# Order of small fp32 products on TensorE in a hybrid decoder step

## The chip, the cores and the metric

The kernel runs on one core of a Trainium2 chip. Its time is what one execution takes on the device, in microseconds (us); the profile is that of one execution, and TensorE, VectorE, ScalarE, GpSimd and SyncE stand in it as PE (PEld for its weight loads), DVE, ACT, POOL and SP.

## What is computed

One layer of a decoder for 1024 new prompt tokens and 64 sampled tokens (8 sequences of 8): a normalised input goes through one projection, whose columns feed an RWKV-7 recurrence (4 heads of 64), a short convolution and a stick-breaking attention (8 heads of 64); then an output projection, an MLP of width 4096 and a gated embedding. The sampled tokens continue 8 cached states and attend to 512 past positions each, kept in pages of 128 rows that a page table names. The parts that bear on the change:

```python
def wkv7_scan(r, decay, k, v, a_vec, b_vec, s0):
    def step(s, inp):
        r_t, w_t, k_t, v_t, a_t, b_t = inp
        sa = jnp.einsum('bhvk,bhk->bhv', s, a_t)
        s = (s * w_t[:, :, None, :] + sa[..., None] * b_t[:, :, None, :]
             + v_t[..., None] * k_t[:, :, None, :])
        y = jnp.einsum('bhvk,bhk->bhv', s, r_t)
        return s, y
...
        z = jnp.einsum('bqhd,bkhd->bhqk', q_blk.astype(jnp.float32), kf) * scale + bias_f
        mask = k_pos[None, :] < q_pos[:, None]
        log_beta = jnp.where(mask, jax.nn.log_sigmoid(z), -jnp.inf)
        log_keep = jnp.where(mask, jax.nn.log_sigmoid(-z), 0.0)
        later = lax.cumsum(log_keep, axis=3, reverse=True) - log_keep
        wts = jnp.exp(log_beta + later)
        return jnp.einsum('bhqk,bkhd->bqhd', wts, vf)
```

## The kernel before

The large products (projections, MLP) split every fp32 operand into a high and a low part and add three full-array products (L169 to L171, L775 to L777, L1262 to L1264). The work that the change touches is done in plain fp32 products whose operands have 64 rows, 64 columns or both. A product `matmul(out, w, x)` loads `w` into the array. The partitions (rows of memory) on which `w` and `x` lie are the array's rows, the partitions of `out` are its columns. So a product whose operands lie on partitions 0 to 63 and whose result goes to partitions 64 to 127 uses one quarter of the array.

The prompt's recurrence runs in chunks of 64 tokens. `wkv_local` does the work of two neighbouring chunks (e = 0, 1) that needs no state, in steps that each fill a PSUM bank and have it evacuated by ScalarE or VectorE: masked products of keys and queries (L507, head halves s = 0, 1 on opposite row halves, all 128 columns), transposes (L514, L522), then four products per chunk, one for each head, in L529, L541, L548, L557, L558 and L569. In L529 to L558 chunk 0 and chunk 1 lie on opposite rows and write opposite halves of a bank; in L569 heads alternate between the column halves. `wkv_chain` carries the state from chunk to chunk: L614 prepares the state's additions, L622 (128 rows) and L624 (64 rows, with the state) accumulate the output of a chunk head by head, L630 carries the state on. `hp(h)` is the half of the partitions that head h uses, `es(e)` and `ks(e)` are the halves that chunk e uses. Two generators of `wkv_local` and one of `wkv_chain` are advanced in turn by `run`; each `wkv_local` generator takes its banks from `banks(3)` or from `banks(4)`, that is, one bank each, and the next taker of a bank waits until it has been read out.

`wkv_sample_chunk` treats the 64 sampled tokens as one chunk with 8 states: it transposes the 8 states of two heads at a time (L698), runs `wkv_local` with a single chunk, adds the states' share of the output (L707 and, 8 per head, L710), and makes the new states (L719, L722, L731, transposes in L738).

`decode` is the paged attention of the sampled tokens: two sequences (s = 0, 1) at a time, whose results go to opposite halves of a bank. Pages are gathered by POOL into rotating buffers (5 for keys, 6 for values), key pages are transposed (L1100), and the scores (L1106, 4 products of 512 columns per sequence, accumulated), the weights (a scan on VectorE) and the values (L1130, one product for each of 4 pages, and L1131 for the new rows, accumulated) follow. L1072 makes the scores of the new rows.

The kernel text gives the order of the program; a scheduler lays the instructions of each engine into a queue from it, taking what it reckons to be ready, so that products of other parts (the query, key and value projection beside the recurrence, the convolution and the first attention beside the sampled chunk, the MLP's first part beside the decode attention) stand between those of a stage. [...]

Of the kernel before, what the change touches and what calls it, by code (L numbers as in the profile page):

```python
# [32 lines left out]
NB = 8  # L33
# [7 lines left out]
PAGES = 4  # L41
# [7 lines left out]
def hybrid_step(ctx: ExitStack, tc: tile.TileContext, I, O):  # L49
# [402 lines left out]
    def hp(h):  # L452
        return slice(64 * (h % 2), 64 * (h % 2) + 64)
# [4 lines left out]
    def j2(t, n=128):  # L458
        return t[:, :n].rearrange("p (j c) -> p j c", j=2)
# [3 lines left out]
    def wkv_local(cs, res, local, sample=False):  # L463
# [5 lines left out]
        def es(e):  # L469
            return slice(64 * e, 64 * e + 64)  # L470
# [28 lines left out]
        mk = mfull[:, 1 if sample else 0].rearrange("p a t -> p (a t)")[:, None, None, :].to_broadcast([128, ne, 2, 128])  # L499
        for s in range(2):  # L500
            hs = slice(64 * s, 64 * s + 64)
            pab = local()
            p4 = pab.rearrange("p (e j c) -> p e j c", e=2, j=2)
            for e in E:
                for j in range(2):
                    ra = ar[hs, e, j, 0:2] if e == 0 else ar[hs, e, j, 2:0:-1]
                    PE.matmul(p4[:, e, j, :], bk[hs, e, j].rearrange("p a t -> p (a t)"), ra, start=True, stop=True)  # L507
            V.tensor_mul(AB[:, 0:ne, s:4:2, 64:192], p4[:, 0:ne], mk)
        yield
# [16 lines left out]
        px = local()  # L526
        for e in E:
            for h in range(4):
                PE.matmul(h4(px)[es(e), h, :], AB[ks(e), e, h, 128:192], UV[ks(e), e, h, :], start=True, stop=True)  # L529
# [3 lines left out]
        if not sample:  # L533
            LM = kp.tile([128, 4, 64], F32, name="LM", bufs=1 if sample else 2)
            for e in E:
                V.tensor_mul(LM[es(e)], AB[es(e), e, :, 128:192], lvl[es(e), None, :].to_broadcast([64, 4, 64]))
            yield
            py = local()
            for e in E:
                for h in range(4):  # L540
                    PE.matmul(h4(py)[es(e), h, :], LM[es(e), h, :], TT[es(e), h, 1, :], start=True, stop=True)  # L541
            Y1 = kp.tile([128, 4, 64], F32, name="Y1", bufs=1 if sample else 2)
            S.copy(Y1, h4(py))
            yield
            pd = local()
            for e in E:
                for h in range(4):
                    PE.matmul(h4(pd)[es(e), h, :], Y1[es(e), h, :], TT[es(e), h, 0, :], start=True, stop=True)  # L548
            V.tensor_add(TT[:, :, 0], h4(pd), TT[:, :, 0])
            yield  # L550
        else:
            yield
        psv = local()
        p4 = h4(psv, 512)
        for e in E:
            for h in range(4):
                PE.matmul(p4[es(e), h, 0:64], TT[es(e), h, 0, :], X[es(e), h, :], start=True, stop=True)  # L557
                PE.matmul(p4[es(e), h, 64:128], TT[es(e), h, 0, :], UV[es(e), e, h, :], start=True, stop=True)  # L558
        for e in E:
# [4 lines left out]
        Rm = kp.tile([128, ne, 2, 64], F32, name="Rm", bufs=1 if sample else 3)  # L564
        FT = kp.tile([128, ne, 2, 64], F32, name="FT", bufs=1 if sample else 3)
        for e in E:
            prf = local()
            for h in range(4):
                PE.matmul(j2(prf, 256)[hp(h), h // 2, :], Wm[es(e), h, :], AB[es(e), e, h, 0:128], start=True, stop=True)  # L569
            V.tensor_add(Rm[:, e], j2(prf, 256)[:, :, 64:128], R(e))  # L570
            if not sample:
                V.tensor_add(FT[:, e], j2(prf, 256)[:, :, 0:64], id128[:, None, :].to_broadcast([128, 2, 64]))
# [33 lines left out]
    def wkv_chain(c, AB, UV, Wm, Rm, FT):  # L606
# [11 lines left out]
        for e in range(2):  # L618
            St = state[0]
            for h in range(4):  # L620
                o = p4[hp(h), e, h // 2, :]
                PE.matmul(o, UV[:, e, h, :], AB[:, e, h, 64:128], start=True, stop=St is None)  # L622
                if St is not None:
                    PE.matmul(o, St[hp(h), h // 2, :], Rm[hp(h), e, h // 2, :], start=False, stop=True)  # L624
            if St is None:
                state[0] = PG[:, e]
                continue
            pf = chain()
            for h in range(4):
                PE.matmul(j2(pf)[hp(h), h // 2, :], FT[hp(h), e, h // 2, :], St[hp(h), h // 2, :], start=True, stop=True)  # L630
            Sn = kp.tile([128, 2, 64], F32, name="St", bufs=3)
            for j in range(2):
                V.scalar_tensor_tensor(Sn[:, j, :], j2(pf)[:, j, :], pcs[:, j, c + e:c + e + 1], PG[:, e, j, :],
                                       op0=ALU.mult, op1=ALU.add)
            state[0] = Sn
            yield
# [13 lines left out]
    def wkv_prompt_chunks():  # L650
# [16 lines left out]
        steps = chains()  # L667
        run(locals_(range(0, 16, 4), banks(3), 0), locals_(range(2, 16, 4), banks(4), 5), steps, steps)
        St = state[0]
# [8 lines left out]
    def wkv_sample_chunk(bank):  # L678
# [12 lines left out]
        for j in range(2):  # L691
            pt = bank()
            s_in = sp.tile([128, NB, 64], F32, name="s_in", tag="um", bufs=2)
            for s in range(2):
                hs = slice(64 * s, 64 * s + 64)
                SP.dma_start(s_in[hs], st[:, 2 * j + s].rearrange("b v k -> v b k"))
                for b in range(NB):
                    PE.matmul(pt[hs, b * 64:b * 64 + 64], s_in[hs, b, :], ident[hs, hs], start=True, stop=True)  # L698
            S.copy(S0[:, j].rearrange("p b v -> p (b v)"), pt)
# [4 lines left out]
        py = bank()  # L704
        for h in range(4):
            o = j2(py)[hp(h), h // 2, :]
            PE.matmul(o, UV[:, 0, h, :], AB[:, 0, h, 64:128], start=True, stop=False)  # L707
            for b in range(NB):
                q = slice(b * NJ, b * NJ + NJ)
                PE.matmul(o[:, q], S0[hp(h), h // 2, b, :], Rm[hp(h), 0, h // 2, q], start=False, stop=b == NB - 1)  # L710
        S.copy(Yg, j2(py))
        run(wkv_out(NP, 64, Yg, bank))
        for j in range(2):
            pg, pf = bank(), bank()
            for s in range(2):
                h = 2 * j + s
                um = sp.tile([128, NB, 64], F32, name="um", tag="um", bufs=2)
                V.tensor_mul(um, UV[:, 0, h, None, :].to_broadcast([128, NB, 64]), bm)
                PE.matmul(pg[hp(h), :], AB[:, 0, h, 0:64], um.rearrange("p b v -> p (b v)"), start=True, stop=True)  # L719
                bmk = sp.tile([64, NB, 64], F32, name="bmk", bufs=1)  # L720
                V.tensor_mul(bmk, AB[0:64, 0, h, None, 0:64].to_broadcast([64, NB, 64]), bm[0:64])
                PE.matmul(pf[hp(h), :], Wm[0:64, h, :], bmk.rearrange("p b k -> p (b k)"), start=True, stop=True)  # L722
# [4 lines left out]
            pn = bank()  # L727
            for s in range(2):
                hs = slice(64 * s, 64 * s + 64)
                for b in range(NB):  # L730
                    PE.matmul(pn[hs, b * 64:b * 64 + 64], FT[hs, b, :], S0[hs, j, b, :], start=True, stop=True)  # L731
            V.tensor_add(GS, pn.rearrange("p (b k) -> p b k", b=NB), GS)
            V.tensor_mul(GS, GS, pcs[:, j, 16:24, None].to_broadcast([128, NB, 64]))
            po = bank()
            for s in range(2):
                hs = slice(64 * s, 64 * s + 64)
                for b in range(NB):
                    PE.matmul(po[hs, b * 64:b * 64 + 64], GS[hs, b, :], ident[hs, hs], start=True, stop=True)  # L738
# [268 lines left out]
    def decode():  # L1007
# [61 lines left out]
        pzn = pdc()  # L1069
        for b in range(NB):  # L1070
            for r in range(4):
                PE.matmul(pzn[64 * (b % 2):64 * (b % 2) + 64, (b // 2) * NS:(b // 2) * NS + NS], Qb[:, r, b, :],  # L1072
                          kT[:, r, :], start=r == 0, stop=r == 3)
# [16 lines left out]
        for bp in range(4):  # L1090
# [11 lines left out]
            pz = pdc()  # L1102
            for s in range(2):
                b = 2 * bp + s
                for r in range(4):
                    PE.matmul(pz[64 * s:64 * s + 64, :], Qb[:, r, b, :], kts[s][:, r, :], start=r == 0, stop=r == 3)  # L1106
            beta = dp.tile([128, W_], F32, name="dbeta", bufs=2)
# [17 lines left out]
            po = pdc()  # L1125
            for s in range(2):
                q = slice(64 * s, 64 * s + 64)
                for n in range(PAGES):
                    vp = page("vpg", vrows, 2 * bp + s, n, 6)
                    PE.matmul(po[q, :], wT[:, n, q], vp, start=n == 0, stop=False)  # L1130
                PE.matmul(po[q, :], wT[:NS, 4, q], vd.rearrange("t r c -> t (r c)"), start=False, stop=True)  # L1131
            ow = dp.tile([128, 8, 64], F32, name="ow", bufs=2)
# [255 lines left out]
```

## Time and profile before

| | us |
|---|---|
| median of 3 runs | 1829.38 |
| lowest and highest of them | 1828.57, 1829.54 |
| the profiled execution | 1823.9 |
| its span | 1822.2 |

The granted TensorE clock of the profiled execution was 0.985 on average. In the lines of a timeline that follow, the columns are the start in us from the span's start, the length in us from the first start to the last end, the engine, the line of the kernel, the operation, result and operands, then the rows and columns of the array used, the moving operand, and the number of records that were merged. The end of a product is modelled, so one lasts longer than the distance to the next start; what a line costs is read from its start to the start of the next line.

### The profile page before, as it was taken

The numbers are of one execution on the slowest core, as the hardware profiler recorded it, in microseconds if no ns is written. First come the engines' busy times: TensorE is split into PE (matmuls) and PEld (weight loads), VectorE is DVE, ScalarE is ACT, GpSimd is POOL, SyncE is SP. The second block draws the span as 40 slices with busy tenths as digits, with TensorE's granted clock in tenths as the row PEclk, the third lists the DMA queues.
The fourth block names the chain that finished last, engine by engine and source line by source line (L and its number), as shares of the span: only waits on it lengthen the run. The fifth ranks groups of instructions, "written<-read, shape, count | busy, mean of one in ns | idle before, by whom it ended". The sixth has DMA issues, their size and how long they took to land.

```text
span 1822.2 us, 29843 instructions
## 1 busy us (share of the span) xinstructions
PE 1761.2 (97%) x11933; PEld 1560.7 (86%) x11933; DVE 1016.2 (56%) x1634; ACT 703.2 (39%) x1283; POOL 480.6 (26%) x412
## 2 busy tenths in 40 slices
PE   6998899999999799999999999999999999999998
PEld 5898888888998777888886665799999999998998
DVE  6267944443566669878763334435555555548532
ACT  5633223222433557565532223334222322225421
POOL 4123321212200243222235433242122212212310
PEclk9999999999989899999999999999999999999999
DMA  5135366423513653333245443523222222221121
GB/s 177 49 121 147 100 154 163 101 71 108 154 50 93 194 168 99 120 119 109 86 120 174 126 126 105 187 70 93 93 72 91 80 84 93 70 87 60 53 72 38
DMA packets 195149, 194.87 MB, mean 107 GB/s; under 512 B 57729, under 2 KB 166945, under 8 KB 194882
## 3 DMA queue, kind: packets, MB, share of 16 engines
q1 hardware_dynamic: 189890, 176.18, 32.4%
q0 software_dynamic: 5120, 16.78, 3.1%
q8 instruction: 94, 1.54, 0.4%
q14 instruction: 45, 0.37, 0.1%
HBM read 155.92 MB, written 36.98 MB: 106 GB/s over the span
## 4 chain that ended last, share of the span: by engine, by line
PE 80%; DVE 9%; DMA 4%; issue 3%; ACT 3%; POOL 1%; SPq 0%; ACTq 0%; DVEq 0%; POOLq 0%
PE b L169 12%; PE b L170 12%; PE b L171 12%; PE b L1262 6%; PE b L1264 6%; PE b L1263 6%; PE b L775 2%; PE b L776 2%; PE b L777 2%; PE b L1130 2%; PE b L895 1%; PE b L1106 1%; DVE base_Q L281 1%; DVE keep L875 1%; DVE nl L1189 1%
## 5 line engine op out<-in xcount | busy, mean ns | idle before, releaser
L159 POOL TENSOR_TENSOR wl<-wr,wh 128x1024 fp32r<-128x1024 f32 (+1 forms) x116 | 289.8, 2517 | 594.0 <-ACT wh L158 593.8
L170 PE MATMUL b<-nl,wh 128*128 128x288 f32 (+1 forms) x960 | 316.7, 330 | 2.2 <-DVE nl L1189 2.2
L169 PE MATMUL b<-nh,wh 128*128 128x288 f32 (+1 forms) x960 | 317.4, 331 | 0.9 <-DVE x L1234 0.9
L171 PE MATMUL b<-nh,wl 128*128 128x288 f32 (+1 forms) x960 | 315.9, 329 | 0.0
L158 ACT CAST wh<-wr 128x1024 fp32r<-128x1024 f32 (+1 forms) x178 | 177.9, 1041 | 265.5 <-PE b L1263 164.1
L1265 DVE TENSOR_TENSOR x<-b,x 128x288 f32<-128x288 f32 (+1 forms) x384 | 200.8, 531 | 140.5 <-PE b L1264 140.3
L1262 PE MATMUL b<-ah,wh 128*128 128x288 f32 (+1 forms) x768 | 256.9, 335 | 5.8 <-DVE x L1265 5.3
L1264 PE MATMUL b<-ah,wl 128*128 128x288 f32 (+1 forms) x768 | 252.3, 329 | 0.0
L1263 PE MATMUL b<-al,wh 128*128 128x288 f32 (+1 forms) x768 | 251.8, 328 | 0.0
L170 PEld LDWEIGHTS b<-nl,wh 128*128 128x128 f32 x960 | 180.9, 188 | 14.9 <-DVE nl L1189 3.1
L169 PEld LDWEIGHTS b<-nh,wh 128*128 128x128 f32 x960 | 180.9, 188 | 14.7 <-issue 1.6
L171 PEld LDWEIGHTS b<-nh,wl 128*128 128x128 f32 x960 | 181.0, 189 | 14.5 <-issue 2.7
L1262 PEld LDWEIGHTS b<-ah,wh 128*128 128x128 f32 x768 | 144.4, 188 | 23.3 <-DVE x L1265 8.2
L1264 PEld LDWEIGHTS b<-ah,wl 128*128 128x128 f32 x768 | 144.4, 188 | 12.2 <-issue 2.4
L1263 PEld LDWEIGHTS b<-al,wh 128*128 128x128 f32 x768 | 144.4, 188 | 9.1 <-issue 0.8
L775 PE MATMUL b<-wh,h_hi 128*128 128x256 f32 x432 | 128.8, 298 | 0.0
L776 PE MATMUL b<-wl,h_hi 128*128 128x256 f32 x432 | 127.9, 296 | 0.0
L777 PE MATMUL b<-wh,h_lo 128*128 128x256 f32 x432 | 127.1, 294 | 0.0
L169 PE MATMUL b<-h_hi,wh 128*128 128x384 f32 (+1 forms) x336 | 116.2, 346 | 1.9 <-ACT xs L330 1.2
L1247 DVE SCALAR_TENSOR_TENSOR r<-b,rb 128x288 f32<-128x288 f32 (+1 forms) x96 | 51.1, 534 | 117.2 <-PE b L171 114.3
L875 DVE TENSOR_TENSOR_SCAN keep<-keep,onesq 128x128 f32<-128x128 f32 (+3 forms) x64 | 97.6, 1528 | 31.9 <-ACT keep L874 31.5
L170 PE MATMUL b<-h_lo,wh 128*128 128x384 f32 (+1 forms) x336 | 113.8, 339 | 0.3 <-DVE h_lo L201 0.3
(375 smaller groups left out, 3427.7 us busy)
## 6 DMA issues: line engine op xcount, KB each, us to landing
wr<-in_w_up SPq DMA_DIRECT2D x62, 512.0 KB
wr<-in_w_down SPq DMA_DIRECT2D x62, 512.0 KB
wr<-in_w_in SPq DMA_DIRECT2D x26, 512.0 KB
wr<-in_w_out SPq DMA_DIRECT2D x16, 512.0 KB
xt<-in_x_prompt SPq DMA_DIRECT2D x8, 512.0 KB
stk_s<-sth SPq DMA_DIRECT2D x32, 128.0 KB
stk_s<-stl SPq DMA_DIRECT2D x32, 128.0 KB
out<-nat SPq DMA_DIRECT2D x16, 256.0 KB
```

Of the source, the lines that this page charges most:

```text
L158: S.copy(wh[:, flat], raw[:, :n * ncol])
L159: (sub or G).tensor_sub(wl[:, flat], raw[:, :n * ncol], f(wh[:, flat]))
L169: PE.matmul(ps[:, :n], wh[:, k, c], a, start=(k == 0), stop=False)
L170: PE.matmul(ps[:, :n], wh[:, k, c], b, start=False, stop=False)
L171: PE.matmul(ps[:, :n], wl[:, k, c], a, start=False, stop=(k == nk - 1))
L775: PE.matmul(o, a, w[0][:, k, :], start=(k == 0), stop=False)
L776: PE.matmul(o, a, w[1][:, k, :], start=False, stop=False)
L777: PE.matmul(o, b, w[0][:, k, :], start=False, stop=(k == 7))
L1262: PE.matmul(ps[:, :n], wh[:, k, c], a, start=k == 0, stop=False)
L1263: PE.matmul(ps[:, :n], wh[:, k, c], b, start=False, stop=False)
L1264: PE.matmul(ps[:, :n], wl[:, k, c], a, start=False, stop=k == 1)
L1265: V.tensor_add(p.x[:, m, t0:t0 + n], ps[:, :n], p.x[:, m, t0:t0 + n])
```

## The change

The order of products changes, so that neighbours use different row halves, different column halves or both. The products themselves and what they compute stay.

- `wkv_local`: L507 alternates between the row halves, with one bank for each (in the sampled chunk it stays one half after the other); L529, L541, L548, L557, L558 run through the heads outside and the chunks inside; in the step of L557 and L558 the two products L557 of a head are neighbours, then the two L558. L569 takes both chunks' banks first and then alternates chunks.
- `wkv_prompt_chunks`: the two generators take banks 3 and 4 in turn from one common cycle.
- `wkv_chain`: the two heads of a pair j first both run L622, then both run L624.
- `wkv_sample_chunk`: L698, L731 and L738 alternate between the halves for each state; the two state loads of a pair stand ahead of all its transposes; L707 and L710 alternate the two heads of a pair; the two masked copies for L719 are both made before its two products, L722 follows.
- `decode`: L1072 and L1106 alternate two sequences for each of the four accumulated parts; the value pages of two sequences are gathered alternately, and L1130 and L1131 alternate the sequences.

```diff
-        for s in range(2):
-            hs = slice(64 * s, 64 * s + 64)
-            pab = local()
-            p4 = pab.rearrange("p (e j c) -> p e j c", e=2, j=2)
+        for both in ((0,), (1,)) if sample else ((0, 1),):
+            p4s = {s: local().rearrange("p (e j c) -> p e j c", e=2, j=2) for s in both}
             for e in E:
                 for j in range(2):
-                    ra = ar[hs, e, j, 0:2] if e == 0 else ar[hs, e, j, 2:0:-1]
-                    PE.matmul(p4[:, e, j, :], bk[hs, e, j].rearrange("p a t -> p (a t)"), ra, start=True, stop=True)
-            V.tensor_mul(AB[:, 0:ne, s:4:2, 64:192], p4[:, 0:ne], mk)
+                    for s in both:
+                        hs = slice(64 * s, 64 * s + 64)
+                        ra = ar[hs, e, j, 0:2] if e == 0 else ar[hs, e, j, 2:0:-1]
+                        PE.matmul(p4s[s][:, e, j, :], bk[hs, e, j].rearrange("p a t -> p (a t)"), ra,
+                                  start=True, stop=True)
+            for s in both:
+                V.tensor_mul(AB[:, 0:ne, s:4:2, 64:192], p4s[s][:, 0:ne], mk)
...
-        for e in E:
-            for h in range(4):
+        for h in range(4):
+            for e in E:
                 PE.matmul(h4(px)[es(e), h, :], AB[ks(e), e, h, 128:192], UV[ks(e), e, h, :], start=True, stop=True)
...
-        for e in E:
-            for h in range(4):
+        for h in range(4):
+            for e in E:
                 PE.matmul(p4[es(e), h, 0:64], TT[es(e), h, 0, :], X[es(e), h, :], start=True, stop=True)
+            for e in E:
                 PE.matmul(p4[es(e), h, 64:128], TT[es(e), h, 0, :], UV[es(e), e, h, :], start=True, stop=True)
...
+        prfs = [local() for e in E]
+        for h in range(4):
+            for e in E:
+                PE.matmul(j2(prfs[e], 256)[hp(h), h // 2, :], Wm[es(e), h, :], AB[es(e), e, h, 0:128],
+                          start=True, stop=True)
         for e in E:
-            prf = local()
-            for h in range(4):
-                PE.matmul(j2(prf, 256)[hp(h), h // 2, :], Wm[es(e), h, :], AB[es(e), e, h, 0:128], start=True, stop=True)
+            prf = prfs[e]
...
-            for h in range(4):
-                o = p4[hp(h), e, h // 2, :]
-                PE.matmul(o, UV[:, e, h, :], AB[:, e, h, 64:128], start=True, stop=St is None)
+            for j in range(2):
+                for h in (2 * j, 2 * j + 1):
+                    PE.matmul(p4[hp(h), e, j, :], UV[:, e, h, :], AB[:, e, h, 64:128], start=True, stop=St is None)
                 if St is not None:
-                    PE.matmul(o, St[hp(h), h // 2, :], Rm[hp(h), e, h // 2, :], start=False, stop=True)
+                    for h in (2 * j, 2 * j + 1):
+                        PE.matmul(p4[hp(h), e, j, :], St[hp(h), j, :], Rm[hp(h), e, j, :], start=False, stop=True)
...
-        run(locals_(range(0, 16, 4), banks(3), 0), locals_(range(2, 16, 4), banks(4), 5), steps, steps)
+        both = banks(3, 4)
+        run(locals_(range(0, 16, 4), both, 0), locals_(range(2, 16, 4), both, 5), steps, steps)
...
             for s in range(2):
-                hs = slice(64 * s, 64 * s + 64)
-                SP.dma_start(s_in[hs], st[:, 2 * j + s].rearrange("b v k -> v b k"))
-                for b in range(NB):
+                SP.dma_start(s_in[64 * s:64 * s + 64], st[:, 2 * j + s].rearrange("b v k -> v b k"))
+            for b in range(NB):
+                for s in range(2):
+                    hs = slice(64 * s, 64 * s + 64)
                     PE.matmul(pt[hs, b * 64:b * 64 + 64], s_in[hs, b, :], ident[hs, hs], start=True, stop=True)
...
-        for h in range(4):
-            o = j2(py)[hp(h), h // 2, :]
-            PE.matmul(o, UV[:, 0, h, :], AB[:, 0, h, 64:128], start=True, stop=False)
+        for j in range(2):
+            for h in (2 * j, 2 * j + 1):
+                PE.matmul(j2(py)[hp(h), j, :], UV[:, 0, h, :], AB[:, 0, h, 64:128], start=True, stop=False)
             for b in range(NB):
                 q = slice(b * NJ, b * NJ + NJ)
-                PE.matmul(o[:, q], S0[hp(h), h // 2, b, :], Rm[hp(h), 0, h // 2, q], start=False, stop=b == NB - 1)
+                for h in (2 * j, 2 * j + 1):
+                    PE.matmul(j2(py)[hp(h), j, q], S0[hp(h), j, b, :], Rm[hp(h), 0, j, q], start=False,
+                              stop=b == NB - 1)
...
-            for s in range(2):
-                b = 2 * bp + s
-                for r in range(4):
-                    PE.matmul(pz[64 * s:64 * s + 64, :], Qb[:, r, b, :], kts[s][:, r, :], start=r == 0, stop=r == 3)
+            for r in range(4):
+                for s in range(2):
+                    PE.matmul(pz[64 * s:64 * s + 64, :], Qb[:, r, 2 * bp + s, :], kts[s][:, r, :], start=r == 0,
+                              stop=r == 3)
...
-            for s in range(2):
-                q = slice(64 * s, 64 * s + 64)
-                for n in range(PAGES):
-                    vp = page("vpg", vrows, 2 * bp + s, n, 6)
+            qs = slice(0, 64), slice(64, 128)
+            for n in range(PAGES):
+                vps = [page("vpg", vrows, 2 * bp + s, n, 6) for s in range(2)]
+                for q, vp in zip(qs, vps):
                     PE.matmul(po[q, :], wT[:, n, q], vp, start=n == 0, stop=False)
+            for q in qs:
                 PE.matmul(po[q, :], wT[:NS, 4, q], vd.rearrange("t r c -> t (r c)"), start=False, stop=True)
```

L541 and L548 change as L529 does; L731 and L738 as L698; L1072 as L1106.

## What is forecast, and from what

> **What bounds the kernel now.** I read three views: the page, for who is busy and what the chain that ended last is made of; the busy time by stretches of the span, for the three stages that the change touches; and TensorE's timeline inside them, for the distance from one start to the next.
>
> ```profile
> span 1822.2 us, 29843 instructions
> ...
> PE 1761.2 (97%) x11933; PEld 1560.7 (86%) x11933; DVE 1016.2 (56%) x1634; ACT 703.2 (39%) x1283; POOL 480.6 (26%) x412
> ...
> PE 80%; DVE 9%; DMA 4%; issue 3%; ACT 3%; POOL 1%; SPq 0%; ACTq 0%; DVEq 0%; POOLq 0%
> ```
> ```profile
> 250.00:460.00 210.00, 206.68 (x2176) 182.87 (x2177) 87.27 (x206) 60.06 (x133) 38.96 (x35) 0.98 0.44 111
> 490.00:606.00 116.00, 112.80 (x816) 100.59 (x815) 71.67 (x134) 48.39 (x112) 8.76 (x31) 0.94 0.28 80
> 606.00:650.00 44.00, 35.89 (x184) 30.99 (x185) 29.97 (x45) 24.46 (x51) 15.67 (x15) 0.88 0.61 186
> 949.00:1150.00 201.00, 198.77 (x841) 123.59 (x841) 70.73 (x83) 59.34 (x99) 79.16 (x73) 0.99 0.44 133
> ```
>
> The columns of the second fence are the stretch, its length, then busy time of PE, PEld, DVE, ACT and POOL, the granted clock, the DMA share and GB/s. TensorE is busy 97% of the span and is 80% of the chain that ended last. In the recurrence of the prompt (250 to 460 us) it is busy 206.7 of 210 us, with the query, key and value products filling every pause; in the decode attention (949 to 1150) 198.8 of 201, with the MLP as filler. What TensorE is spared there comes off the end. In the sampled chunk (490 to 606) it is busy 112.8 of 116, but the 44 us behind it leave TensorE 8 us of waits: what is spared there is partly lost in them.
>
> A busy share does not tell whether products overlap. The starts do:
>
> ```profile
> 272.01 0.96 PE L529 MATMUL b<-UV,AB 64*64 64x64 f32 x16
> 272.90 0.66 PE L522 MATMUL b<-ident,ar 128*128 128x128 f32 x4
> ```
> ```profile
> 108.70 2.20 PE L260 MATMUL b<-sigw,kn 64*64 64x64 f32 x68
> ```
> ```profile
> 545.32 1.08 PE L719 MATMUL b<-um,AB 128*64 128x512 f32 x4
> 546.33 0.44 PE L895 MATMUL b<-ident,beta 128*128 128x128 f32 x2
> ```
> ```profile
> 574.37 1.07 PE L719 MATMUL b<-um,AB 128*64 128x512 f32 x2
> 575.37 0.50 PE L869 MATMUL b<-stk_k,stk_q 128*128 128x512 f32 x1
> ```
>
> A plain fp32 product leaves two records: L529 has 8 products in 16 records. The time to the next line's start is its price: 0.89 us for 8, 0.11 each, where four in a row use the same 64 rows and columns of the array. L260 computes products of the same shape, but each neighbour takes the other 64 rows and the other 64 columns: 34 products, and from the first start to the last (2.20 less the 0.22 that a single one lasts) 33.5 steps of **0.059 us**. So neighbours on disjoint parts already run two at a time. At 512 columns it holds too, with disjoint columns alone: L719's two products into the two halves of a bank take 1.01 us together (545.32 to 546.33), and one such product alone takes 1.00 us (574.37 to 575.37).
>
> ```profile
> 348.04 0.34 PE L614 MATMUL b<-UV,AB 128*64 128x64 f32 x4
> 348.31 0.65 PE L569 MATMUL b<-AB,Wm 64*64 64x128 f32 x8
> ```
>
> **The change, part by part.** No product is added or removed; the sum is over places where neighbours become disjoint. Two disjoint L614 take 0.27 us with the switch to the next shape, which is 2 x 0.059 + 0.15. So for a group of n disjoint 64-column products I take 0.059 n + 0.15 us.
>
> *Prompt recurrence.* 16 chunks make 8 groups of two.
>
> ```profile
> 260.54 1.49 PE L507 MATMUL b<-ar,bk 64*128 64x128 f32 x16
> 261.97 0.39 PE L775 MATMUL b<-wh,h_hi 128*128 128x256 f32 x1
> ```
> ```profile
> 294.10 1.16 PE L507 MATMUL b<-ar,bk 64*128 64x128 f32 x8
> 295.18 0.33 PE L622 MATMUL b<-AB,UV 128*64 128x64 f32 x2
> 295.44 0.33 PE L624 MATMUL b<-Rm,PG 64*64 64x64 f32 x2
> 295.69 0.33 PE L622 MATMUL b<-AB,UV 128*64 128x64 f32 x2
> ```
> ```profile
> 324.44 0.28 PE L558 MATMUL b<-UV,TT 64*64 64x64 f32 x2
> 324.56 0.28 PE L557 MATMUL b<-X,TT 64*64 64x64 f32 x2
> ```
>
> L507: four products of one row half take 1.08 us (294.10 to 295.18), so a group costs 2.16. Alternating halves, eight should take the time of four: 1.08 saved, 8 times, **8.6**. The nearest row is the run of eight at 260.54, two halves in a row, 1.43: bound 0.73 x 8 = 5.8. L529, L541 and L548: 24 groups of eight, 0.89 to 8 x 0.059 + 0.15 = 0.62: **6.5**. L557 and L558: starts are 0.12 apart (324.44, 324.56), 16 products 1.87; paired 1.09: 0.78 x 8 = **6.2**. L569 alternates columns already, and I count nothing.
>
> L622 and L624 alternate between 128 and 64 rows, 0.26 us each (295.18, 295.44, 295.69): four pairs of them in a step of the state are 2.05. The change puts two L622 on the two column halves together, then two L624 on opposite quarters. Two such neighbours cost 0.27 with the switch behind them, so a step is 4 x 0.27 = 1.06 and saves 0.99, over the 15 steps with a state 14.8. But a first L622 is often issued alone and the last L624 already overlaps the following line, so I count three quarters: **11.1**, and 6 as the lower bound. Together 32.4 us.
>
> This part also takes a wait: the two generators of local work had one PSUM bank each (3 and 4) and now share both. Behind a blocked product on TensorE's in-order queue stand the filler products. I cost it at nothing, because TensorE has the filler to run; its price without that cover is a rival below.
>
> *Sampled chunk.* One chunk, so L507 to L569 gain nothing.
>
> ```profile
> 487.67 1.90 PE L698 MATMUL b<-ident,s_in 64*64 64x64 f32 x32
> 489.50 0.33 PE L871 MATMUL b<-later,ident_r 128*128 128x128 f32 x1
> ```
> ```profile
> 524.55 0.33 PE L707 MATMUL b<-AB,UV 128*64 128x64 f32 x2
> 524.81 1.09 PE L710 MATMUL b<-Rm,S 64*64 64x8 f32 x16
> 525.84 0.33 PE L707 MATMUL b<-AB,UV 128*64 128x64 f32 x2
> ```
>
> L698, L731 and L738: 16 products in 1.83 us each, two runs of each; paired 16 x 0.059 + 0.15 = 1.09: 0.74 x 6 = 4.4. L707 and L710: 0.26 + 1.03 per head, 5.2 for four; paired 2 x (0.27 + 1.04) = 2.6: saves 2.6. L719's second pair runs apart (574.37) and would run together: 1.0. Sum 8.0; for the waits behind the stage I count **4**, bounds 0 and 8. The state loads on SP's queue now stand together ahead of the transposes; those ran as one block already, so nothing moves there.
>
> *Decode.*
>
> ```profile
> 959.01 3.65 PE L1106 MATMUL b<-KT,Qb 128*64 128x512 f32 x8
> 962.59 0.50 PE L171 MATMUL b<-nh,wl 128*128 128x512 f32 x1
> ```
> ```profile
> 994.51 3.65 PE L1130 MATMUL b<-vpg,wT 128*64 128x512 f32 x8
> 998.08 1.07 PE L1131 MATMUL b<-d,wT 64*64 64x512 f32 x2
> 999.08 1.93 PE L1130 MATMUL b<-vpg,wT 128*64 128x512 f32 x4
> 1000.94 1.09 PE L1100 MATMUL b<-ident,kpg 128*128 128x128 f32 x8
> 1005.40 1.07 PE L1130 MATMUL b<-vpg,wT 128*64 128x512 f32 x2
> 1007.52 1.07 PE L1130 MATMUL b<-vpg,wT 128*64 128x512 f32 x2
> ```
>
> L1106: four products of one sequence take 3.58 us, eight groups 28.6. Paired, eight take what four took; the first may go out before the second sequence's keys are there, for which I add 0.5: 4 x 4.08 = 16.3, **12.3** saved, bounds 10 and 14.3. L1130 and L1131: a pair of sequences costs 3.57 + 1.00 + 1.86 + 1.00 + 1.00 + 1.00 = 9.4 (the last two pages and the last L1131 each alone). Six page buffers now hold three pages of both sequences; the fourth pages still wait for a buffer, on POOL's queue ahead of further gathers and of the splitting of weights, no longer than now, since the same first products release them. So three pairs run at 0.86 with 0.14 around them (2.7), two late pages alone (2.0) and one pair of L1131 (1.0): 5.7, saving 3.7 x 4 = **15**, bounds 9 (all pages apart, only L1131 and half of the pairs joined) and 20 (all paired). L1072 is small and left out. Together 27.3.
>
> **Sum:** 32.4 + 4 + 27.3 = 63.7 us. The profiled execution took 1823.9 with its span of 1822.2, the median of the three runs is 1829.4, 5.5 more; the saving does not depend on that difference, so 1829.4 - 64 = **1765 us**. With every upper bound (14.8 for 11.1, 8 for 4, 14.3 and 20) it is 1829.4 - 78 = 1751; with every lower one (5.8, 6, 0, 10, 9 and the two sums of 6.5 and 6.2) 1829.4 - 44 = 1786.
>
> **The rivals.** *Neighbours do not stay neighbours*: the instruction scheduler issues what is ready and puts filler between. For it speaks that one sequence's L1106 ran as a block of four at 959.01, not waiting for the other's. Against it: every later L622 of a step needs no state, yet stands behind the L624 ahead of it (295.18 to 295.69), so products into one tile keep their order. If half of the pairs break, 64 becomes 32: 1797 us.
>
> *The trace's pairs with disjoint columns alone were an accident*, and only disjoint rows let two products overlap. Then L1106, L1130, L1131, L719 and the L622 half of the recurrence gain nothing: 64 - 27.3 - 1 - 5.5 = 30, 1799 us. L719's 1.01 us for two speaks against it.
> [...]
>
> *Two row halves may not share a bank*: L529 to L558, L624, L698 and the like write both halves of one bank. If that serialised them, 6.5 + 6.2 + 5.5 + 2 = 20 us fall away: 1785.
> [...] L260 does it, at 0.059 us a product, so the trace disagrees.
>
> *Slower: the shared banks.* One generator's next product waits until the other's is evacuated.
>
> ```profile
>   DVE AB L508: 34.2, 12
> ```
>
> Each group takes a bank ten times, 80 in all over two banks, 40 one after another. VectorE waited 34.2 us in 12 times for L507, so a hand-over of 2 to 3 us is usual, 40 x 2.9 = 116 us, inside the stage's 210. It decides when the stage outlasts its filler by more than the 31 us of the other two parts: 40 hand-overs would have to take (210 + 31) / 40 = 6.0 us each. At 6.5 the stage ends at 250 + 260 = 510 instead of 460, and the time is 1829 + 50 - 31 = 1848.
>
> *Nothing to measure*: spared TensorE time comes back as waits for weights or for VectorE, 1829. In the decode POOL is busy 79 of 201 us and DMA 0.44, which speaks against it.
>
> **How the numbers follow.** My forecast 0.63, broken neighbours 0.18, columns that do not pair 0.03, rows that share no bank 0.03, nothing 0.05, slower 0.08. Three runs of before lie within 0.1% of each other, so about 0.2% (3.7 us) is the least that can be told from no change. Faster is the first four, 0.87; same 0.05; slower 0.08. The range goes from the best sum, 1751, a little rounded down, to past broken neighbours: 1750 to 1800.
>
> **What would show it.** Right: L1106 in runs of 14 to 16 records in about 3.6 us; L507 16 records in about 1.1; L529 16 in about 0.6; L622 and L624 in groups of four records of 0.27; the query, key and value products ending some 30 us earlier, decode ending 60 us earlier. Wrong: these groups cut by filler, 0.43 us between L1106's starts with no pair, or TensorE idle in 250 to 460 us behind evacuations of banks 3 and 4.

## The result, and the profile after

| | before | after |
|---|---|---|
| median of the runs, us | 1828.97 (4 runs, 1819.62 to 1829.54) | 1770.65 (4 runs, 1763.51 to 1776.06) |
| ratio, 95% interval | | 0.969, 0.9642 to 0.9739 |
| the profiled execution, us | 1823.9 | 1768.19 |
| its span, us | 1822.2 | 1766.5 |

58.3 us less by the medians, 55.7 by the spans of the two profiled executions; 64 were forecast. One execution of the kernel before, beside runs 1 to 4, took 4295.91 us and is left out of every figure below. From here the lines of the changed kernel have its own numbers: L507 is L508, L529 is L532, L541 L544, L548 L551, L557 L560, L558 L562, L569 L573, L614 L621, L622 L629, L624 L632, L630 L638, L698 L708, L707 L717, L710 L721, L1072 L1087, L1100 L1115, L1106 L1120, L1130 L1145, L1131 L1147. L775 to L777, the projection that fills the recurrence's pauses, are L790 to L792. The table of lines and the account of the prediction name the terms by the numbers of before.

The page of the changed kernel, and its busy time by roughly the same four stretches of work as before (stretch, length, busy time of PE, PEld, DVE, ACT and POOL, granted clock, DMA share, GB/s):

```profile
PE 1700.9 (96%) x11933; PEld 1522.0 (86%) x11933; DVE 1013.9 (57%) x1634; ACT 702.3 (40%) x1283; POOL 484.9 (27%) x412
```
```profile
250.00:432.00 182.00, 175.84 (x2131) 155.79 (x2130) 85.30 (x201) 57.56 (x128) 38.95 (x35) 0.97 0.50 128
467.00:572.00 105.00, 103.20 (x845) 91.17 (x845) 70.59 (x131) 48.23 (x111) 8.08 (x29) 0.98 0.30 86
572.00:620.00 48.00, 40.62 (x208) 34.70 (x207) 31.07 (x49) 27.63 (x56) 16.16 (x17) 0.89 0.62 193
915.00:1102.00 187.00, 181.61 (x878) 123.44 (x877) 73.97 (x91) 61.20 (x101) 82.78 (x76) 0.98 0.48 144
```

The same 11933 products are there, and TensorE still bounds: 96% busy. All three stages are shorter: the recurrence, from the first L507 to the last L630, took 200.4 us before and 177.0 after; the sampled chunk, from the first L698 to the last L738, 114.4 and 102.5; the decode, from the first L1072 to the last L1131, 199.6 and 183.9. The stretch behind the sampled chunk leaves TensorE 7.4 us of waits, where it left 8.1, and the other engines' busy times have hardly moved. TensorE's timeline of the changed kernel shows why the stages are shorter:

```profile
337.01 0.34 PE L629 MATMUL b<-AB,UV 128*64 128x64 f32 x4
337.27 0.33 PE L632 MATMUL b<-Rm,St 64*64 64x64 f32 x4
...
338.20 1.15 PE L532 MATMUL b<-UV,AB 64*64 64x64 f32 x32
339.28 0.70 PE L591 MATMUL b<-Yg,bones 128*128 128x256 f32 x2
...
503.31 1.10 PE L721 MATMUL b<-Rm,S 64*64 64x8 f32 x32
504.35 0.34 PE L717 MATMUL b<-AB,UV 128*64 128x64 f32 x4
...
984.63 1.07 PE L1120 MATMUL b<-KT,Qb 128*64 128x512 f32 x2
985.63 0.50 PE L1278 MATMUL b<-ah,wh 128*128 128x512 f32 x1
...
989.94 3.65 PE L1120 MATMUL b<-KT,Qb 128*64 128x512 f32 x14
993.51 0.50 PE L1278 MATMUL b<-ah,wh 128*128 128x512 f32 x1
```

Two L629 take 0.26 us (337.01 to 337.27) where one took 0.26. Sixteen L532 of two groups take 1.08 us (338.20 to 339.28), 0.067 each with the switch, against 0.11. L721 is through with two heads in 1.04 us (503.31 to 504.35); one head took 1.03. And seven L1120 take 3.57 us where four took 3.58, once the lone first has gone out at 984.63. But not every line pairs:

```profile
253.45 0.73 PE L508 MATMUL b<-ar,bk 64*128 64x128 f32 x8 [2.37 <-DMA bk<-bk_s]
254.11 0.39 PE L791 MATMUL b<-wl,h_hi 128*128 128x256 f32 x1
...
272.74 1.16 PE L508 MATMUL b<-ar,bk 64*128 64x128 f32 x8
273.82 0.38 PE L790 MATMUL b<-wh,h_hi 128*128 128x256 f32 x1
```

Four L508 take 0.66 us in the first group. In six of the other seven groups they go out as two runs of four with other products between, and a run takes 1.08 us, as before (1.52 in one case, in part at half the clock). The seventh is one run of eight in 1.42 us, like the one at 260.54 us before. So only the first group alternates between the two banks.

Summing over a line the time from each record's start to the next one's, in the two traces, gives what each line occupies TensorE for, in us (differences are taken before rounding):

| lines | before | after | spared | forecast |
|---|---|---|---|---|
| L507 | 18.9 | 17.5 | 1.5 | 8.6 |
| L529, L541, L548 | 22.2 | 13.0 | 9.2 | 6.5 |
| L557, L558 | 15.6 | 9.5 | 6.2 | 6.2 |
| L622, L624 | 25.8 | 16.0 | 9.8 | 11.1 |
| L698, L731, L738 | 11.0 | 6.7 | 4.2 | 4.4, half counted |
| L707, L710 | 7.3 | 2.6 | 4.7 | 2.6, half counted |
| L719 | 3.0 | 3.0 | 0 | 1.0, half counted |
| L1106 | 28.6 | 18.3 | 10.3 | 12.3 |
| L1130, L1131 | 37.8 | 22.0 | 15.8 | 15 |

With 0.6 for L1072 and 0.7 for L569, L614 and L630 that is 63.0 us; the forecast's sum was 63.7. The span is 55.7 shorter, so some 7 us came back on other lines. Part of it are waits of TensorE, in the views of its waits from 250 us to the decode's end, before and after:

```profile
PE b L1100 <- DMA kpg<-in_cache_k,idx: 2.2, 2, 1.6
```
```profile
PE b L1115 <- DMA kpg<-in_cache_k,idx: 5.4, 3, 3.6
PE b L790 <- ACT nat L797: 3.7, 1, 3.7
```

The gathered key pages were waited for 5.4 us instead of 2.2, and a bank of the projection 3.7 us for ScalarE, which is new: 6.9 us of these two kinds, against some that became shorter.

### The profile page after: what moved, and what is told of

It is laid out like the page before. It is cut to its first block, busy times and chain, and to the rows that moved or that the text cites. A ratio compares the mean times of both kernels' runs of the same rounds, so it can differ in the third digit from the quotient of the medians.

```text
span 1766.5 us, 29840 instructions
## 1 busy us (share of the span) xinstructions
PE 1700.9 (96%) x11933; PEld 1522.0 (86%) x11933; DVE 1013.9 (57%) x1634; ACT 702.3 (40%) x1283; POOL 484.9 (27%) x412
## 4 chain that ended last, share of the span: by engine, by line
PE 56%; DVE 3%; DMA 2%; POOL 1%; issue 1%; ACT 0%; SPq 0%; ACTq 0%; POOLq 0%; DVEq 0%
PE b L170 10%; PE b L171 10%; PE b L169 10%; PE b L1278 6%; PE b L1279 6%; PE b L1280 6%; PE b L910 1%; DVE nl L1205 1%; PE b L1145 1%; PE b L1120 1%; PE b L1115 1%; DMA kpg<-in_cache_k,idx 1%; PE b L921 1%; PE b L920 1%; DVE x L1281 1%
## 5 line engine op out<-in xcount | busy, mean ns | idle before, releaser
L171 PEld LDWEIGHTS b<-nh,wl 128*128 128x128 f32 x960 | 180.4, 188 | 12.7 <-issue 0.8
L1280 PEld LDWEIGHTS b<-ah,wl 128*128 128x128 f32 x768 | 144.5, 188 | 10.2
L790 PE MATMUL b<-wh,h_hi 128*128 128x256 f32 x432 | 129.4, 300 | 3.7 <-ACT nat L797 3.7
L792 PE MATMUL b<-wh,h_lo 128*128 128x256 f32 x432 | 127.0, 294 | 0.0
L171 PE MATMUL b<-h_hi,wl 128*128 128x384 f32 (+1 forms) x336 | 112.5, 335 | 0.0
```

The costliest lines, as they stand in the source:

```text
L171: PE.matmul(ps[:, :n], wl[:, k, c], a, start=False, stop=(k == nk - 1))
L790: PE.matmul(o, a, w[0][:, k, :], start=(k == 0), stop=False)
L792: PE.matmul(o, b, w[0][:, k, :], start=False, stop=(k == 7))
L1280: PE.matmul(ps[:, :n], wl[:, k, c], a, start=False, stop=k == 1)
```

## The experiments

For runs 1 to 11 I give beside the median the mean time of a kernel's executions, the mean of the granted TensorE clocks that each execution recorded (1 is full speed), and the product of time and clock per execution, averaged. TensorE is busy for 96% of the span, so an execution that was granted 1% less clock takes close to 1% longer. The 85 executions of the table bear this out: within a kernel, 0.01 less clock went with about 15 us more, 0.85%. The product is a rough measure of the work with that taken out. It scatters by 2 to 3 us from one execution to the next, so a difference of two of these averages is known to about 1.5 us.

| kernel | median us | ratio to before, 95% | mean us | clock | product |
|---|---|---|---|---|---|
| before, beside runs 1 to 4 | 1827.78 | | 1829.2 | 0.9826 | 1797.4 |
| 1 decode alone | 1810.62 | 0.989, 0.984 to 0.9939 | 1811.4 | 0.9795 | 1774.2 |
| 2 chain alone | 1810.70 | 0.9885, 0.985 to 0.992 | 1810.6 | 0.9868 | 1786.6 |
| 3 sampled chunk alone | 1814.83 | 0.9912, 0.988 to 0.9943 | 1815.1 | 0.9867 | 1790.9 |
| 4 local products alone | 1811.20 | 0.989, 0.9854 to 0.9925 | 1810.8 | 0.9867 | 1786.8 |
| before, beside runs 5 to 8 | 1824.91 | | 1825.0 | 0.9845 | 1796.6 |
| 5 changed kernel | 1773.24 | 0.9712, 0.9682 to 0.9742 | 1772.4 | 0.9832 | 1742.6 |
| 6 old L507, own banks | 1763.34 | 0.9663, 0.9634 to 0.9692 | 1764.0 | 0.9882 | 1743.1 |
| 7 pairs of L507 forced | 1763.74 | 0.9663, 0.9636 to 0.9691 | 1764.3 | 0.9865 | 1740.4 |
| 8 decode in full pairs | 1767.19 | 0.9677, 0.9643 to 0.971 | 1765.7 | 0.9830 | 1735.6 |
| before, beside runs 9 to 11 | 1825.84 | | 1826.6 | 0.9844 | 1798.1 |
| 9 old L507, shared banks | 1765.49 | 0.9662, 0.9643 to 0.9682 | 1766.2 | 0.9860 | 1741.5 |
| 10 run 6 and full pairs | 1758.19 | 0.9631, 0.9613 to 0.9649 | 1758.5 | 0.9866 | 1735.0 |
| 11 run 7 and full pairs | 1756.93 | 0.961, 0.9588 to 0.9633 | 1756.0 | 0.9864 | 1732.1 |

**Runs 1 to 4: each part alone.** The edits are the parts of the change's diff: that of `decode`; that of `wkv_chain`; that of `wkv_sample_chunk`; those of L529 to L558 in `wkv_local`.

> The kernel before with the decode edits alone (L1072, L1106, L1130, L1131; L1072 stays L1072 here). Theory, spared TensorE slots are spared time: the profile of the whole change shows 0.6 + 10.3 + 11.8 + 4.0 = 26.7 us less from start to start on these lines, so about 27 us below the kernel before, ratio 0.985. Rival, products that share their rows and differ in columns alone do not overlap: no change. Rival, the decode stage waits for pages anyway and only more filler is done in it: still 27 us, but the stage itself shortens by less than that.

> The kernel before with the two heads' L622 and then their two L624 as neighbours, nothing else. Theory: 6.2 + 3.6 us of slots, and L614 and L630 around them 0.3, so 10 us below the kernel before, ratio 0.9945; runs of four records at 0.265 us. Rival, the recurrence of the prompt is held up by its chain of waits and not by TensorE: within 3 us of the kernel before.

> The kernel before with the edits of the sampled chunk alone. Theory: slots of 0.8 + 3.9 + 1.2 + 1.5 + 1.5 = 8.9 us are spared and nothing of it is lost behind the stage: 9 us below the kernel before, ratio 0.995. Rival, as the prediction counted: half is lost in the waits behind the stage, 4 to 5 us.

> The kernel before with L529, L541, L548, L557 and L558 alone reordered, each generator with its own bank as before. Theory: 2.6 + 2.5 + 2.6 + 2.9 + 3.2 = 13.8 us of slots, ratio 0.9925. Rival, part of the gain of the whole change comes from the shared banks or from another order of the filler: less than 10 us.

Measured by the medians: 17, 17, 13 and 17 us, 64 together, where the whole change gives 52 to 58; the first is less than expected, the other three are more. On their own lines the four spare 26.7, 10.3, 9.0 and 12.2 us, and the whole change spares 26.7, 9.8, 9.0 and 15.4 there. What differs most is the clock. Run 1 was granted 0.9795, runs 2 to 4 0.987, the kernel before 0.9826. Run 1's profiled execution shows it. Up to the end of the sampled chunk its TensorE instructions stand in the order of before, and yet the recurrence took 210.6 us from its first L507 to its last L630, 10 more than before. One stretch of time in it, by the busy time view (first before, then run 1), and run 1's timeline there:

```profile
412.00:424.00 12.00, 12.00 (x141) 10.48 (x138) 6.44 (x15) 4.04 (x9) 2.75 (x3) 1.00 0.18 46
```
```profile
412.00:424.00 12.00, 12.00 (x70) 10.01 (x70) 4.14 (x9) 1.75 (x4) 0.00 (x0) 0.58 0.24 66
```
```profile
413.32 0.33 PE L622 MATMUL b<-AB,UV 128*64 128x64 f32 x2
413.58 0.33 PE L624 MATMUL b<-Rm,St 64*64 64x64 f32 x2
413.84 0.48 PE L622 MATMUL b<-AB,UV 128*64 128x64 f32 x2
...
416.23 1.60 PE L548 MATMUL b<-TT,Y 64*64 64x64 f32 x16
417.76 0.91 PE L811 MATMUL b<-ident,nat 128*128 128x128 f32 x3
```

TensorE is busy without a break, but its clock falls to half at 413.84 (0.50 from 414 to 424 us), after a run of single L622 and L624. Eight L548 then take 1.53 us (416.23 to 417.76) instead of 0.89. Taken by the products, the four parts give 23.2, 10.8, 6.5 and 10.6 us, 51.1 together, and the whole change 54.0 (1796.6 to 1742.6). So the parts add. The rival that columns alone give no overlap falls with run 1, and the rival that the chain's waits bound the recurrence falls with run 2. Run 1's second rival holds as to the stage: the decode stage is 15.0 us shorter (199.6 to 184.6, first L1072 to last value product), less than its lines spare, and the MLP's products in it take 61.2 us instead of 53.4.

For the sampled chunk the runs do not decide between all and half: 13 by the medians, 6.5 by the products, 9.0 on its lines. Part of the 9.0 is the clock. Run 1 leaves L707 and L710 as they were, and in its profile, at a granted clock of 1.00, they take 5.2 us instead of the 7.3 in the profile before. At full clock the change thus spares 2.6 us on these two lines and 6.8 on all lines of the chunk. In the changed kernel's profile the stage shrank by 11.9 us, but its granted clock rose from 0.94 to 0.98; length times clock fell by 7 us (107.5 to 100.5). The time from there to the decode's first L1072 stayed (346.9 and 346.4, at 0.98 and 0.99), so there nothing was lost.

**Runs 5, 6 and 9: L507 and the shared banks.** Run 6 takes back three places of the change:

```diff
-        for both in ((0,), (1,)) if sample else ((0, 1),):
-            p4s = {s: local().rearrange("p (e j c) -> p e j c", e=2, j=2) for s in both}
+        for s in range(2):
+            hs = slice(64 * s, 64 * s + 64)
+            pab = local()
...
-        prfs = [local() for e in E]
...
-        both = banks(3, 4)
-        run(locals_(range(0, 16, 4), both, 0), locals_(range(2, 16, 4), both, 5), steps, steps)
+        run(locals_(range(0, 16, 4), banks(3), 0), locals_(range(2, 16, 4), banks(4), 5), steps, steps)
```

Run 9 takes back the first two and keeps the common cycle of banks 3 and 4.

> The changed kernel once more, as the measure for the three that follow on the same chip: 58 us below the kernel before, ratio 0.968.

> The changed kernel with L507, L569 and the banks as before (one bank for each generator). Theory: in the changed kernel only one of eight groups of these products was interleaved, so undoing it costs 1.5 + 0.4 = 2 us of slots: within 5 us of the changed kernel, ratio to before 0.969. Rival, the shared banks cost waits that hide a gain: 5 to 10 us faster than the changed kernel. Rival, the shared banks help the local steps beyond the products' order: over 5 us slower.

> The changed kernel with L507 and L569 in the order of before, but the two generators taking banks 3 and 4 in turn from one cycle, as in the changed kernel. The run with its own bank for each generator was 10 us faster than the changed kernel. Theory, taking turns is what costs, since a generator's next step waits for the other's evacuation: as slow as the changed kernel, 1770 to 1775 us. Rival, what costs is that L507 holds both banks while its two halves go out apart: as fast as with own banks, 1760 to 1766.

The changed kernel was 52 us below before, not 58. Run 6 came out 10 us faster than it, and run 9 nearly as much, which by the expectations says that not the taking of turns costs, but L507 holding both banks while its halves go out apart. I do not call that shown. The three products are 1742.6, 1743.1 and 1741.5, no difference; the 10 us go with a clock of 0.9832 against 0.9882 and 0.9860. The changed kernel's ten executions lie between 0.980 and 0.987, run 6's six between 0.986 and 0.991, so the lower clock belongs to the kernel more than to chance; which of its instructions bring it about stays open. What is settled is that L507's part of the change gains nothing that these runs can tell, as only the first of eight groups alternates.

**Run 7: the pairs of L507 forced.**

```diff
             p4s = {s: local().rearrange("p (e j c) -> p e j c", e=2, j=2) for s in both}
+            if not sample:
+                V.memset(p4s[1][0:1, 0, 0, 0:1], 0.0)
+                V.tensor_copy(p4s[0][0:1, 0, 0, 0:1], p4s[1][0:1, 0, 0, 0:1])
             for e in E:
```

> The changed kernel with two one-element VectorE instructions ahead of each group of L507 (a zero written into the second bank, copied into the first), so that no product of the group can go before both banks are free. Theory, the order was lost to the readiness of the first bank: all eight groups interleave, eight products take 1.1 to 1.3 us instead of 2.17, 17.5 us of slots become 10 to 11, and the kernel is 6 to 7 us faster than the changed one. Rival, products that differ in rows alone and write two banks overlap only partly: runs of 1.4 us, 4 us at most. Rival, waiting for both banks costs what the pairs spare: no change.

Now no product is ready before both banks are. All eight groups alternate. A later group in run 7's timeline (L511 is L507 there):

```profile
291.88 1.16 PE L511 MATMUL b<-ar,bk 64*128 64x128 f32 x16
292.98 0.39 PE L793 MATMUL b<-wh,h_hi 128*128 128x256 f32 x1
```

Eight products in 1.10 us, against the 1.08 of the prediction, so these products, which differ in rows alone and write two banks, overlapped fully. The line's total is 11.3 us, against 17.5 in the changed kernel. The kernel is 9.5 us faster than run 5 by the medians, but at a higher clock, and 2.2 by the products, which is hardly told from nothing. So by the products most of the 6.2 us spared on the line was given back elsewhere; in run 7's profile the recurrence lasts 197.5 us instead of 177.0, with more filler done in it. The rival of no change is not far off.

**Run 8: the decode in full pairs.**

```diff
             for r in range(4):
-                for s in range(2):
+                for s in (1, 0):
                     PE.matmul(pz[64 * s:64 * s + 64, :], Qb[:, r, 2 * bp + s, :], kts[s][:, r, :], start=r == 0,
...
-                vps = [page("vpg", vrows, 2 * bp + s, n, 6) for s in range(2)]
+                vps = [page("vpg", vrows, 2 * bp + s, n, 8) for s in range(2)]
```

> The changed kernel with the second sequence ahead of the first in L1106, so that the first product waits for the later keys, and eight instead of six buffers for value pages (the buffers of dbeta and ow go from two to one to make room). Theory: the lone first product costs 1.00 instead of 0.43 us in each of four pairs of sequences, the late value pages 2.0 instead of 0.86: 2.3 + 4.6 = 7 us less, scores in runs of 16 records of 3.6 us, values and new rows in one run of about 4.5. Rival, the stage is held up by the page gathers, so that the products only move: runs as said, and under 3 us.

The changed kernel's values of one pair of sequences, and then run 8's scores and values, in the timelines:

```profile
961.62 2.80 PE L1145 MATMUL b<-vpg,wT 128*64 128x512 f32 x12
964.34 1.53 PE L1115 MATMUL b<-ident,kpg 128*128 128x128 f32 x12
...
972.49 1.07 PE L1145 MATMUL b<-vpg,wT 128*64 128x512 f32 x2
973.49 1.08 PE L1147 MATMUL b<-d,wT 64*64 64x512 f32 x4
974.50 0.50 PE L170 MATMUL b<-nl,wh 128*128 128x512 f32 x1
```
```profile
953.35 3.65 PE L1120 MATMUL b<-KT,Qb 128*64 128x512 f32 x16
956.94 0.50 PE L1278 MATMUL b<-ah,wh 128*128 128x512 f32 x1
...
970.73 3.65 PE L1145 MATMUL b<-vpg,wT 128*64 128x512 f32 x16
974.31 1.07 PE L1147 MATMUL b<-d,wT 64*64 64x512 f32 x4
975.32 0.87 PE L1115 MATMUL b<-ident,kpg 128*128 128x128 f32 x6
```

The first is the prediction's own picture: three pairs of pages in 2.72 us, a page alone, its partner late, in 1.00, and one pair of new rows in 1.01. In run 8 the scores go out as one run of 16 records in 3.59 us and the values and new rows in 4.59. The kernel is 6.0 us faster than run 5 by the medians and 7.0 by the products; 7 were expected.

**Runs 10 and 11: the two together.**

> The changed kernel with L507, L569 and banks as before, and with the decode in full pairs (second sequence first in L1106, eight buffers for value pages). Theory, the two gains are in stages apart and add: 1763 - 6 = 1757 us, ratio 0.963. Rival, the 10 us between own and shared banks were a chance of the runs: 1765 us.

> The changed kernel with the forced pairs of L507 and the decode in full pairs. Theory, the gains add: 1764 - 6 = 1758 us, ratio 0.963. Rival, the forced pairs gain nothing over own banks because the stage waits: no faster than the run with own banks.

1758.19 and 1756.93 us: both as expected. Run 11, with a ratio of 0.961 (0.9588 to 0.9633) against the changed kernel's 0.9712 (0.9682 to 0.9742), has the lowest median of this study; between 10 and 11 the intervals do not decide. By the products the full pairs spare 8.1 us on run 6 and 8.3 on run 7.

**Run 12: pairs broken where the change touches nothing.** In the kernel before, two lines that paired:

```diff
-            for c in range(n):
-                for s in range(2):
+            for s in range(2):
+                for c in range(n):
...
-            for h in range(4):
+            for h in (0, 2, 1, 3):
                 PE.matmul(g4[hp(h), e, h // 2, :], AB[:, e, h, 0:64], UV[:, e, h, :], start=True, stop=True)
```

> The kernel before with two lines put in an order that breaks their pairs, no other change: L260 runs through all chunks of one half and then of the other, L614 takes the heads in the order 0, 2, 1, 3. Theory, order alone decides: the runs of L260 (34 products in 2.13 us) become 3.3 to 3.7 us, and the four of them 2 to 3 us longer together, less if the two halves overlap where they meet; L614's eight products go from 0.52 to 0.75 us or more. Rival, the pairs come from the shape and not from the order: 2.13 and 0.52 stay.

It was executed once, in 1821.64 us, which cannot show 2 to 3 us; the distances in its timeline can:

```profile
110.03 3.52 PE L260 MATMUL b<-sigw,kn 64*64 64x64 f32 x68
113.49 0.29 PE L337 MATMUL b<-ident,raw 128*9 128x128 f32 x1
...
287.58 0.73 PE L614 MATMUL b<-UV,AB 128*64 128x64 f32 x16
288.10 0.28 PE L622 MATMUL b<-AB,UV 128*64 128x64 f32 x2
...
349.03 0.45 PE L614 MATMUL b<-UV,AB 128*64 128x64 f32 x4
349.40 0.65 PE L569 MATMUL b<-AB,Wm 64*64 64x128 f32 x8
```

The 34 products of L260 take 3.46 us instead of 2.13, so order decides. The second half was a miss: eight L614 in the order 0, 2, 1, 3 still take 0.52 us. Only two of them alone, now on the same half, take 0.37 instead of 0.27, so the queue did hold the order 0, 2, 1, 3. Why the eight lose nothing is not shown: the records do not name the half that a product uses.

## Why the prediction was right, point by point

- **TensorE as the bound of the prompt's recurrence and of the decode**: held. 63.0 us spared on the changed lines became 55.7 us of span; the 7 us between came back on other lines, in part as waits for key pages and for ScalarE.
- **0.059 us a product and 0.15 for the switch**: held. Sixteen L532 at 1.08 us; 16 x 0.059 + 0.15 = 1.09.
- **L507, 8.6 us**: the step that failed. It measured 1.5. I had weighed that neighbours do not stay neighbours, and set against it that products into one tile keep their order. But L507's two halves write two tiles, one in each bank, and this evidence does not reach them: the scheduler issued each bank's four as it came free. Run 7 shows that the 1.08 us for eight paired products was right, with 1.09 to 1.10.
- **L529 to L558**: 15.4 spared for 12.7 forecast. L548's part holds a wait of 1.6 us that the trace of before had ahead of L541 and that is gone.
- **L622 and L624, 11.1**: measured 9.8; the three quarters were a fair choice.
- **The sampled chunk, 4 of 8**: 9.0 on its lines, 6.8 at equal clock, and nothing lost behind it in the profile; the halving had no support there. L707 and L710 gave 4.7 instead of 2.6 because of the clock: the row that I quoted for them was the fastest of four, the one at full clock, and at full clock 2.6 is right. In the profile before, the clock was 0.65 around them, after 1.00:

```profile
524.00:533.00 9.00, 9.00 (x79) 8.30 (x78) 6.98 (x10) 2.80 (x8) 0.39 (x4) 0.65 0.29 88
```
```profile
502.00:511.00 9.00, 9.00 (x114) 8.31 (x113) 8.32 (x14) 3.98 (x10) 0.39 (x4) 1.00 0.29 90
```

  L719's 1.0 did not come: its second pair still goes out 4 us apart.
- **L1106, 12.3, and L1130 with L1131, 15**: 10.3 and 15.8. A lone first product costs 1.00, not the 0.5 that I had added, which is the 2 us.
- **The slower rival**: the shared banks cost no wait of 6 us a hand-over; runs 6 and 9 have the same product of time and clock. The two rivals that speak against columns alone and against row halves in one bank fell with L1120's 3.57 us for seven and with L532's 1.08 for sixteen.
- **The sum** was near in part by luck: L507's 7 us too many stood against the 5 us too few in the sampled chunk, 2 of them from the clock, and 2.7 in L529 to L558. The 7 us that came back on other lines had no term.

## What to carry to other kernels

Where TensorE bounds and many products use half of its rows or columns, compare the distance between starts with that of a line whose neighbours are disjoint: the price of the pair stood in the trace before anything was changed, 0.059 us a product in L260 against 0.11 in L529. Then ask whether the neighbours will be ready together: here the order written in the program held where both products write one tile (sixteen L532 in 1.08 us), but with two banks that came free at different times only one of eight groups of L507 alternated, and a page that came late left a product alone, at 1.00 us. And set the granted clock of each execution beside its time before explaining a difference of half a per cent: runs 5 and 6 lie 10 us apart with clocks of 0.9832 and 0.9882, and their products of time and clock are 1742.6 and 1743.1.

## What the runs showed of the hardware

- The clock fell while TensorE was busy. In run 1 it was at 0.50 from 414 us for 10 us, and TensorE was busy in all of the 12 us from 412 us on. The same instructions ran at 1.00 before, where the clock stays at 1.00 from 260.5 to 502.5 us. In the traces of before and of the changed kernel the stretches at half clock last 3.4, 6.8 or 10.2 us, but for the one that the end of each span cuts. What brings the half clock, and why one execution drops where another does not, no run here shows.
- A waiting product held up those behind it on TensorE. In the profile before, TensorE stood idle for 2.72 us ahead of the first L507 (251.72 us), which waited for the load of `bk`. The next L776 went out only behind it, at 252.10 us, though the L775 of the same sum had started at 248.71 and the last weights for it had been split by 239.9.
- Neighbours on one half did not always cost time: in run 12 eight L614 in the order 0, 2, 1, 3 took the same 0.52 us as in 0, 1, 2, 3, though two of them alone took 0.37 instead of 0.27, and 34 L260 with eight of one half in a row took 3.46 instead of 2.13.
